# Six pairs instead of four: merged sums on VectorE and a four-slot tile of raw weights in an encoder layer

## The chip, the core and the metric

The kernel runs on one core of a Trainium2 chip. The metric is the device time of one execution in microseconds. TensorE (PE), VectorE (DVE), ScalarE (ACT) and the queue of SyncE (SP), which issues nearly all transfers, work side by side and wait for each other by semaphores. Each takes its own instructions strictly in the order in which the program wrote them.

## What is computed

One encoder layer on x of 256 x 4096. Its two large products are what counts here:

```python
h = layer_norm(x, emb_ln_g, emb_ln_b)
p = h @ w_in                      # 4096 x 13312
y_conv = c_b * centred_short_conv(c_c * c_h, conv_w) * silu(c_z)
y_attn = banded_window_attention(a_q, a_k, a_v, sink) * silu(a_z)
y = concatenate([y_conv, y_attn]) @ w_out     # 4096 x 4096
out = layer_norm(DN_ALPHA * h + y, ln_g, ln_b)
```

All is float32. The attention has 16 query heads in 4 groups and a window of 128 positions to each side.

## The kernel before

**Halves.** A float32 product is made of fast matmuls on rounded numbers. ACT rounds the raw weights `w` to `whi` (`split_hi`, L205), DVE subtracts to get the remainder `wlo` (`split_lo`, L209), and PE sums three products: both halves of x with `whi`, the high half of x with `wlo`. There are three buffers of each half, so PE must have finished a step's matmuls before the halves of the step three later can be made.

**Pieces and pairs.** The weights come in steps. A piece ("s") holds four tiles of 128 rows by 512 columns, 1 MB, and costs PE 48 matmuls of 256 columns (`mm`, L252 for the input, `mm_out`, L926 for the output). A pair ("S") holds two such tiles, 0.5 MB, and uses Strassen's scheme: seven products instead of eight, hence 21 matmuls instead of 24 (`mm_pair`, L277 to L280). For that it needs sums of its weight blocks, which DVE makes (`sums`, L184 to L186: one sum of 512 elements a partition, two of 256), and then halves of seven blocks, 1792 elements, instead of 2048 for a piece. It also needs sums of x or y, made once (`x_sums`, `y_sums`), and the four combined results of a chunk are put together by DVE afterwards (`pair_copy`, `pair_sums`, L682 to L685, then `plus_res`, L934).

**Order of the work.** All engines' orders are written by hand. There is a list of steps, first 26 input chunks, then 9 output chunks (seven of 512 columns, numbered 0 to 6 here, and two of 256, numbers 7 and 8). Input chunks from the fourth on have the pattern `sSShSsSSsSSs` (h is half a piece). Output chunks 0 and 1 have eight pieces, chunks 2 to 6 have `sSsSsSsSss`: six pieces and four pairs. In the round of step j the program writes, in this order: the matmuls of step j, `split_hi` of step j+3, whatever else is due there (the table `later`, filled by `at`), the loads, `sums` of step j+4, and `split_lo` of step j+3.

**Loads.** `loads` gives SP the next weights, at most up to step j+7, if a buffer is free by then: `w0` to `w2`, an extra one in the input part, and idle parts of the result tile `R` in the output part. SP waits for DVE to have split what the buffer held.

**Around an output chunk's start.** When the last matmul of a chunk is done, DVE adds its two results to the residual and takes statistics (`end_out`, L941 and L944). In the first step of the next chunk it multiplies them by the last norm's weight (`end_out2`, L948), which frees the tile `gb`; then SP loads the residual rows of the new chunk (`res_load`, L897 to L901: three rows spread over the partitions into `gb`, two tiles of x into `xc`, 256 KB each). DVE prepares them later in the chunk (`residual`, L907 and L909). In chunk 2, `rows_split` also makes 15 small transfers (L876).

**Attention.** In the input part, PE multiplies the softmax's p, turned and split into halves, with v (`pv`, L621 and L623). DVE makes the low half (`p_lo`, L614).

Of the kernel before, what the change touches and what calls it, by code (L numbers as in the profile page):

```python
# [27 lines left out]
PIECE = HK * P  # L28
# [4 lines left out]
W = 512  # L33
# [7 lines left out]
HW = W // 2  # L41
# [47 lines left out]
def npairs(ci):  # L89
    return PAIRS[ci] if ci < OUT else OUT_ORDERS[ci - OUT].count("S")  # L90

# [3 lines left out]
N_IN = len(IN_STEPS)  # L95
# [6 lines left out]
def encoder_kernel(ctx: ExitStack, tc: tile.TileContext, x, emb_g, emb_b, wi, ws, conv_w, sink, wo, ln_g, ln_b, out):  # L102
    nc = tc.nc
# [20 lines left out]
    raw, wh, wl = {}, {}, {}  # L124
    psc = pw = pc = R = None
    extra = []
    user = {}
    in_R = [(steps.index(("opair", OUT + 4, OP - 1)) + 1, "R0"), (steps.index(("opair", OUT + 4, OP - 1)) + 1, "R1"),
            (steps.index(("opair", OUT + 6, OP - 1)) + 1, "R2")]

    def w_bufs(j):

        bs = [(wpool, f"w{k}") for k in range(N_W)] + (extra if j < N_IN else [])
        if j >= N_IN and R is not None:
            late = j > in_R[0][0]
            bs += [(None, name) for last, name in in_R if j <= last and late == (name == "R2")]
        last_user = lambda b: max(u for c, u in user.items() if c == b or b[1] == "R2" and c[0] is None) if (
            b in user or b[1] == "R2") else -1
        return min((last_user(b), k) for k, b in enumerate(bs)), bs

    def load(j, to=None):
        kind, a, b = steps[j]
        if to is None:
            (_, k), bs = w_bufs(j)
            pool, name = bs[k]
            user[bs[k]] = j
            if pool is None:
                to = raw[j] = {"R0": R[:, 0, D // 2:D], "R1": R[:, 1, D // 2:D], "R2": R[:, :, 3 * D // 4:D]}[name]
            else:
                to = raw[j] = pool.tile([P, PIECE], F32, name=name, bufs=1)  # L150
        src = {"in": (wi, IN_PIECES), "out": (wo, OUT_PIECES)}.get(kind, (ws, ALL_PAIRS))
        src = src[0][src[1].index((a, b))]
        if len(to.shape) == 3:
            if is_pair(j):
                nc.sync.dma_start(out=to[:, 0, :], in_=src)
            else:
                nc.sync.dma_start(out=to, in_=src.rearrange("p (i n) -> p i n", i=2))
        else:
            nc.sync.dma_start(out=to[:, 0:src.shape[1]], in_=src)

    def loads(j):

        nonlocal nxt
        while nxt < len(steps) and nxt <= j + 7:
            (u, _), bs = w_bufs(nxt)
            if u > j + (2 if len(bs) > N_W else 3):
                break
            load(nxt)
            nxt += 1

    def sums(j):
# [12 lines left out]
        nc.vector.tensor_tensor(s01, b22, b12.to_broadcast([P, 2, HW]), op=ALU.add)  # L184
        nc.vector.tensor_tensor(r(6), r(5), r(1), op=ALU.add)  # L185
        nc.vector.tensor_tensor(r(7), r(6), r(3), op=ALU.add)  # L186
# [7 lines left out]
    def half_tile(j, name):  # L194
        if j < len(steps) - 1 and name == "whi":
            return wpool.tile([P, PIECE + GAP], F32R, name=name)[:, OFF:OFF + PIECE]
        if j < len(steps) - 1:
            return wpool.tile([P, PIECE + 2 * OFF], F32R, name=f"{name}{j % 3}", bufs=1)[:, OFF:OFF + PIECE]
        (_, k), bs = w_bufs(j)
        user[bs[k]] = j  # L200
# [29 lines left out]
    for name in ("whi", "w0", "w1", "w2", "wlo0", "m", "nm", "wlo1", "den", "es", "wlo2"):  # L230
        n = {"whi": PIECE + GAP}.get(name, PIECE + 2 * OFF if name[:3] == "wlo" else PIECE if name[0] == "w" else 2)
        wpool.tile([P, n], F32, name=name, bufs={"whi": 3, "m": 4, "nm": 3, "den": 4, "es": 3}.get(name, 1))


    acc = {}
# [58 lines left out]
    with tc.tile_pool(name="pro", bufs=1) as pro:  # L294
# [28 lines left out]
        for j in range(4, 2 + N_W):  # L323
            load(j)

        NQ = KT // 4
# [99 lines left out]
        x_split(3)  # L426
        split(3)
        load(6)
        transp2(4)
        mm(2)  # L430
        turned2(4)
        x_split(4)
        split(4)
        load(7)
        transp2(5)
        mm(3)
        turned2(5)
        x_split(5)
        split(5)
        load(8)  # L440
        transp2(6)
        mm(4)
        turned2(6)
        x_split(6)
        split(6)
        load(9)
        transp2(7)
        mm(5)
        turned2(7)
        x_split(7)  # L450
        split(7)
        load(10)
        mm(6)
        split(8)
        load(11)
        x_split(0)
        split(9)
        load(12)
        x_split(1)
    n_pro = 7  # L460

# [300 lines left out]
    def at(j, fn, *a):  # L762
        later.setdefault(j, []).append((fn, a))
# [33 lines left out]
                at(j + t, f, g, b)  # L797

    c_ch0 = IN_ORDER.index(C_CH)
    nxt = n_pro + 6  # L800
# [61 lines left out]
    first_cols, zt = [], []  # L862

    def rows_load():
        for k, src in enumerate((ln_g, ln_b)):
# [12 lines left out]
    def res_load(n):  # L878
# [5 lines left out]
        if n < ncs - 2:  # L884
            xc = p2.tile([P, 2, W], F32, name="xc")[:, :, 0:w]
        elif n == ncs - 2:
            zt.append(p2.tile([P, 8 * W], F32, name="z", tag="SC"))
            xc = zt[0][:, 6 * W:6 * W + 2 * w].rearrange("p (a b) -> p a b", a=2)
        else:
            z = zt[0]  # L890
            gb = z[:, 0:3 * w].rearrange("p (a b) -> p a b", a=3)
# [246 lines left out]
```

## Time and profile before

| | us |
|---|---|
| median of three runs | 1503.43 (1503.41 to 1503.45) |
| the profiled execution's own time | 1503.42 |
| its span, first to last instruction | 1501.7 |
| PE busy, share of the span | 1488.7 (99%) |
| DVE busy | 1329.3 (89%) |
| ACT busy | 782.0 (52%) |
| granted TensorE clock, mean | 0.999 |

Rows of a timeline read: start in us, duration in us, engine, line, operation, tiles written and read, shape, count, and in brackets the idle time before it and what ended that. Rows of groups give, after the shape and count, the total busy time in us, the mean of one in ns, and the idle time before them with its releasers. "w<-in_ws" is the transfer of a pair's weights, "w<-in_wi" and "w<-in_wo" those of pieces.

### The profile page before, as it was taken

To read this page: it belongs to the slowest core of one execution; us is meant where nothing else is said; L and a number is where in the kernel's file an instruction comes from. 1 tells how busy PE (TensorE), PEld (TensorE's weight loads), DVE (VectorE), ACT (ScalarE), POOL (GpSimd) and SP (SyncE) were. 2 spreads that over 40 slices of the span, in tenths; PEclk is the share of its full clock that TensorE was granted. 3 is DMA by queue.
4 is the path that set the end of the run, shared out by engine and by line. 5 is a ranking of instruction groups with operands and counts; after the bars stand their busy time and mean duration, and the time that the engine had idled before them with its cause. 6 is when DMAs were issued, how large, how long until landed. Compare 5 with 4: busy or idle time off the path is not lost.

```text
span 1501.7 us, 30113 instructions
## 1 busy us (share of the span) xinstructions
PE 1488.7 (99%) x12947; PEld 1473.4 (98%) x12947; DVE 1329.3 (89%) x1555; ACT 782.0 (52%) x669; POOL 1.3 (0%) x7
## 2 busy tenths in 40 slices
PE   7999999999999999999999999999999999999998
PEld 4999999999999999999999999999999999999997
DVE  7768989999899998999899999999999688888876
ACT  5545556657566665544555455555455444444431
POOL 0000000000000000000000000000000000000000
PEclk9999999999999999999999999999999999999999
DMA  7555655656555556657556655656667665666673
GB/s 290 217 182 197 210 197 172 208 185 205 200 184 190 190 185 212 230 188 241 202 191 210 225 201 193 216 185 228 203 211 292 259 204 219 262 218 217 221 260 124
DMA packets 71749, 316.18 MB, mean 211 GB/s; under 512 B 8544, under 2 KB 12608, under 8 KB 50880
## 3 DMA queue, kind: packets, MB, share of 16 engines
q1 hardware_dynamic: 70608, 312.43, 59.5%
q8 instruction: 101, 1.65, 0.4%
q10 hardware_dynamic: 1008, 1.84, 0.3%
q14 instruction: 32, 0.26, 0.1%
HBM read 305.23 MB, written 8.91 MB: 209 GB/s over the span
## 4 chain that ended last, share of the span: by engine, by line
PE 98%; DVE 1%; DMA 0%; ACT 0%; SPq 0%; issue 0%; ACTq 0%
PE acc L252 45%; PE acc L926 20%; PE pacc L278 6%; PE pacc L277 6%; PE pacc L280 6%; PE acc L278 4%; PE acc L277 4%; PE acc L280 4%; PE att L494 1%; DVE st L331 0%; PE att L621 0%; PE att L607 0%; PE acc L381 0%; DMA x<-in_x 0%; PE att L364 0%; DVE x L339 0%
## 5 line engine op out<-in xcount | busy, mean ns | idle before, releaser
L205 ACT ACTIVATE whi<-w 128x2048 fp32r<-128x2048 f32 (+1 forms) x354 | 621.9, 1761 | 590.7 <-DVE w L186 230.4
L209 DVE TENSOR_TENSOR wlo<-w,whi 128x2048 fp32r<-128x2048 f32 (+1 forms) x354 | 736.0, 2083 | 101.0 <-ACT whi L205 84.0
L252 PE MATMUL acc<-whi,xT 128*128 128x256 f32 x3952 | 473.4, 276 | 0.0
L252 PEld LDWEIGHTS acc<-whi,xT 128*128 128x128 f32 x3952 | 459.3, 188 | 0.0
L252 PE MATMUL acc<-wlo,xT 128*128 128x256 f32 x1976 | 245.8, 275 | 0.0
L252 PEld LDWEIGHTS acc<-wlo,xT 128*128 128x128 f32 x1976 | 234.0, 188 | 0.0
L926 PE MATMUL acc<-whi,xT 128*128 128x256 f32 x1696 | 201.8, 275 | 0.0
L926 PEld LDWEIGHTS acc<-whi,xT 128*128 128x128 f32 x1696 | 196.6, 188 | 0.4 <-issue 0.4
L184 DVE TENSOR_TENSOR w<-w 128x512 f32<-128x512 f32 x179 | 122.3, 683 | 7.8 <-DMA w<-in_ws 7.8
L926 PE MATMUL acc<-wlo,xT 128*128 128x256 f32 x848 | 105.3, 275 | 0.0
L277 PE MATMUL acc<-whi,xT 128*128 128x256 f32 x370 | 101.9, 275 | 0.0
L278 PE MATMUL acc<-whi,xT 128*128 128x256 f32 x370 | 101.9, 275 | 0.0
L926 PEld LDWEIGHTS acc<-wlo,xT 128*128 128x128 f32 x848 | 100.4, 188 | 0.0
L277 PE MATMUL pacc<-whi,xT 128*128 128x256 f32 x350 | 97.9, 280 | 0.0
L278 PE MATMUL pacc<-whi,xT 128*128 128x256 f32 x350 | 96.4, 275 | 0.0
L280 PE MATMUL pacc<-wlo,xT 128*128 128x256 f32 x350 | 96.2, 275 | 0.0
L280 PE MATMUL acc<-wlo,xT 128*128 128x256 f32 x370 | 92.8, 275 | 0.0
L277 PE MATMUL pacc<-whi,SC 128*128 128x256 f32 x330 | 90.9, 275 | 0.0
L278 PE MATMUL pacc<-whi,SC 128*128 128x256 f32 x330 | 90.9, 275 | 0.0
L280 PE MATMUL pacc<-wlo,SC 128*128 128x256 f32 x330 | 82.9, 276 | 0.0
L185 DVE TENSOR_TENSOR w<-w 128x256 f32<-128x256 f32 x179 | 76.1, 425 | 6.2
L186 DVE TENSOR_TENSOR w<-w 128x256 f32<-128x256 f32 x179 | 76.1, 425 | 6.2
(218 smaller groups left out, 1673.4 us busy)
## 6 DMA issues: line engine op xcount, KB each, us to landing
w<-in_wi SPq DMA_DIRECT2D x112, 1024.0 KB
w<-in_ws SPq DMA_DIRECT2D x202, 512.0 KB
w<-in_wo SPq DMA_DIRECT2D x41, 1024.0 KB
R<-in_wo SPq DMA_DIRECT2D x13, 1024.0 KB
x<-in_x SPq DMA_DIRECT2D x7, 512.0 KB
yl<-yd SPq DMA_DIRECT2D x7, 512.0 KB
xc<-in_x SPq DMA_DIRECT2D x14, 256.0 KB
R<-in_ws SPq DMA_DIRECT2D x6, 512.0 KB
```

The source lines that it names most:

```text
L184: nc.vector.tensor_tensor(s01, b22, b12.to_broadcast([P, 2, HW]), op=ALU.add)
L185: nc.vector.tensor_tensor(r(6), r(5), r(1), op=ALU.add)
L186: nc.vector.tensor_tensor(r(7), r(6), r(3), op=ALU.add)
L205: nc.scalar.activation(part(j, wh[j]), part(j, raw[j]), AF.Copy)
L209: nc.vector.tensor_tensor(part(j, wl[j]), part(j, raw[j]), part(j, wh[j]).bitcast(F32), op=ALU.subtract)
L252: nc.tensor.matmul(acc[ci, i][:, c:c + HW], x, w[:, k * W + c:k * W + c + HW], start=(first and w is hi and k + off + c == 0), stop=(last ...
L277: nc.tensor.matmul(o, ah, hi[:, w, :], start=(opens and p == 0), stop=False)
L278: nc.tensor.matmul(o, al, hi[:, w, :], start=False, stop=False)
L280: nc.tensor.matmul(o, ah, lo[:, w, :], start=False, stop=(closes and last))
L494: nc.tensor.transpose(ps[:, c, i * P:(i + 1) * P], t[:, i, (2 * b + c) * P:(2 * b + c + 1) * P], ident)
L926: nc.tensor.matmul(acc[ci, i][:, c:c + HW], y, m[:, k * w + c:k * w + c + HW], start=(first and off + c == 0), stop=(last and c + HW == w))
```

## The change

1. Output chunks 2 to 6 have the pattern `sSSsSSsSSss`: five pieces and six pairs (`OP`, `OUT_ORDERS`). The sums of y for six pairs are made in the rounds of steps 6 to 11 of the output part, where those for four were made in steps 9 to 12. Their tile and the tile `z` in the same place grow from 8 to 12 blocks of 512 columns.
2. The three buffers of raw weights become one tile `wall` with four slots. Two pairs that follow each other directly (`couple`) may be loaded into slots only, and their sums are then made together, once, in the round in which those of the first were due: one sum over 2 x 512 elements, two over 2 x 256 (new L192 to L194).
3. A load may go ahead if the step that holds its buffer is at most two steps on, in the prologue three (before, two where there were extra buffers and three elsewhere). In the prologue each load from the seventh on comes one place sooner.
4. The last piece of all is loaded into the tile `z`, and its halves lie in the place of `wall`.
5. The kernel is built with a smaller scratch area for dynamic transfers.

```diff
-OP = 4
-OUT_ORDERS = ["s" * 8] * 2 + ["sSsSsSsSss"] * 5 + ["", ""]
-N_W = 3
+OP = 6
+OUT_ORDERS = ["s" * 8] * 2 + ["sSSsSSsSSss"] * 5 + ["", ""]
+N_W = 4
...
+    def couple(j):
+        return is_pair(j) and j + 1 < len(steps) and is_pair(j + 1) and not (j and couple(j - 1))
+
+    coupled = lambda j: couple(j) or j > 0 and couple(j - 1)
...
-        bs = [(wpool, f"w{k}") for k in range(N_W)] + (extra if j < N_IN else [])
+        bs = [("wall", k) for k in range(N_W)]
+        if coupled(j):
+            return min((user.get(b, -1), k) for k, b in enumerate(bs)), bs
+        bs += extra if j < N_IN else []
...
-            (u, _), bs = w_bufs(nxt)
-            if u > j + (2 if len(bs) > N_W else 3):
+            (u, _), bs = w_bufs(nxt) if nxt < len(steps) - 1 else ((-1, 0), [])
+            if u > j + (2 if j >= n_pro else 3):
                 break
...
     def sums(j):
 
-        if j >= len(steps) or not is_pair(j):
+        if j >= len(steps) or not is_pair(j) or j in summed:
+            return
+        if coupled(j) and j + 1 in in_wall:
+            summed.add(j + 1)
+            a, b = sorted((in_wall[j], in_wall[j + 1]))
+            t = wall[:, a:b + 1:b - a, :].rearrange("p s (b w) -> p s b w", w=HW)
+            nc.vector.tensor_tensor(t[:, :, 4:6, :], t[:, :, 1:3, :], t[:, :, 0:1, :].to_broadcast([P, 2, 2, HW]), op=ALU.add)
+            nc.vector.tensor_tensor(t[:, :, 6, :], t[:, :, 5, :], t[:, :, 1, :], op=ALU.add)
+            nc.vector.tensor_tensor(t[:, :, 7, :], t[:, :, 6, :], t[:, :, 3, :], op=ALU.add)
             return
...
-        return bs[k][0].tile([P, PIECE], F32R, name=bs[k][1], bufs=1)
+        t = wpool.tile([P, 2, 2 * PIECE], F32R, name="wend", tag="wall", bufs=1) if name == "whi" else last_half[0]
+        last_half.append(t)
+        return t[:, int(name == "wlo"), OFF:OFF + PIECE]
...
-        p2.tile([P, 8 * W], F32, name="SC")
+        p2.tile([P, 12 * W], F32, name="SC")
...
     for k in range(OP):
-        at(chunks[1][3] + 1 + k, y_sums, k)
+        at(N_IN + 6 + k, y_sums, k)
...
-    nc = _bacc.Bacc("TRN2", target_bir_lowering=False, num_devices=1)
+    nc = _bacc.Bacc("TRN2", target_bir_lowering=False, num_devices=1, dynamic_dma_scratch_size=1024)
```

**DVE at the start of output chunk 5.** Rows are line, operation, tiles written and read, shape. `wlo` of 1792 are the halves of pairs, of 2048 those of pieces; L948, in the new file L976, is `end_out2`, L944 the end of `end_out`. Before:

```order
L944 BN_STATS s_13769<-R 128x6
L209 TENSOR_TENSOR wlo_15866<-w_15685,whi 128x1792
L948 TENSOR_TENSOR R<-R,gb 128x512 x2
L184 TENSOR_TENSOR w_15801<-w_15801 128x512
L185 TENSOR_TENSOR w_15801<-w_15801 128x256
L186 TENSOR_TENSOR w_15801<-w_15801 128x256
L209 TENSOR_TENSOR wlo_15907<-R,whi 128x2048
L209 TENSOR_TENSOR wlo_15960<-w_15801,whi 128x1792
L184 TENSOR_TENSOR w_15902<-w_15902 128x512
```

After:

```order
L194 TENSOR_TENSOR wall<-wall 128x2x256
L230 TENSOR_TENSOR wlo_15394<-R,whi 128x2048
L976 TENSOR_TENSOR R<-R,gb 128x512 x2
L230 TENSOR_TENSOR wlo_15430<-wall,whi 128x1792
L230 TENSOR_TENSOR wlo_15457<-wall,whi 128x1792
L192 TENSOR_TENSOR wall<-wall 128x2x512
L193 TENSOR_TENSOR wall<-wall 128x2x256
L194 TENSOR_TENSOR wall<-wall 128x2x256
L230 TENSOR_TENSOR wlo_15513<-wall,whi 128x2048
```

Two halves of pairs now follow `end_out2` directly, and then the merged sums of the third couple (steps 7 and 8 of the chunk).

**SP at the same place.** `in_ws` are a pair's weights, `in_wo` a piece's; `gb` and `xc` are the residual loads. Before:

```order
L159 DMA w_15864<-in_wo 128x2048
L897 DMA gb<-in_emb_g_row 128x512
L898 DMA gb<-in_emb_b_row 128x512
L899 DMA gb<-in_ln_g 128x512
L901 DMA xc<-in_x 128x512 x2
L159 DMA w_15902<-in_ws 128x1024
L157 DMA R<-in_wo 128x2x1024
```

After:

```order
L172 DMA wall<-in_ws 128x1024
L925 DMA gb<-in_emb_g_row 128x512
L926 DMA gb<-in_emb_b_row 128x512
L927 DMA gb<-in_ln_g 128x512
L929 DMA xc<-in_x 128x512 x2
L172 DMA wall<-in_ws 128x1024
L170 DMA R<-in_wo 128x2x1024
```

The load in front of the residual loads is now the first pair of the third couple (step 7), the one behind them its second (step 8); before, the load behind them was the pair of step 7, the last of the four.

**DVE in the attention part**, around the later of two low halves of p near the end of a group of heads (`kp<-att,kp`, L614, in the new file L638). Before:

```order
L627 TENSOR_TENSOR zT<-att,zT 128x256
L184 TENSOR_TENSOR w_3445<-w_3445 128x512
L185 TENSOR_TENSOR w_3445<-w_3445 128x256
L186 TENSOR_TENSOR w_3445<-w_3445 128x256
L209 TENSOR_TENSOR wlo_3549<-w_3409,whi 128x2048
L614 TENSOR_TENSOR kp<-att,kp 128x512
L184 TENSOR_TENSOR w_3488<-w_3488 128x512
```

After:

```order
L651 TENSOR_TENSOR zT<-att,zT 128x256
L192 TENSOR_TENSOR wall<-wall 128x2x512
L193 TENSOR_TENSOR wall<-wall 128x2x256
L194 TENSOR_TENSOR wall<-wall 128x2x256
L230 TENSOR_TENSOR wlo_3451<-wall,whi 128x2048
L638 TENSOR_TENSOR kp<-att,kp 128x512
L230 TENSOR_TENSOR wlo_3485<-wall,whi 128x1792
```

The sums of the later pair, which stood behind the low half, are now made together with those of the earlier one in front of it.

More of the change, by code (lines that the diff above doesn't have):

```diff
@@ L142, in load @@
         kind, a, b = steps[j]
-        if to is None:
+        if to is None and j == len(steps) - 1:
+            to = raw[j] = z_tile()[:, 8 * W:12 * W]
+        elif to is None:
             (_, k), bs = w_bufs(j)
@@ L146, in load @@
             user[bs[k]] = j
-            if pool is None:
+            if pool == "wall":
+                to = raw[j] = wall[:, name, :]
+                in_wall[j] = name
+            elif pool is None:
                 to = raw[j] = {"R0": R[:, 0, D // 2:D], "R1": R[:, 1, D // 2:D], "R2": R[:, :, 3 * D // 4:D]}[name]
@@ L229, in encoder_kernel @@
     const.tile([P, 8], F32, name="gap")
-    for name in ("whi", "w0", "w1", "w2", "wlo0", "m", "nm", "wlo1", "den", "es", "wlo2"):
-        n = {"whi": PIECE + GAP}.get(name, PIECE + 2 * OFF if name[:3] == "wlo" else PIECE if name[0] == "w" else 2)
-        wpool.tile([P, n], F32, name=name, bufs={"whi": 3, "m": 4, "nm": 3, "den": 4, "es": 3}.get(name, 1))
+    for name in ("whi", "wall", "wlo0", "m", "nm", "wlo1", "den", "es", "wlo2"):
+        n = {"whi": PIECE + GAP}.get(name, PIECE + 2 * OFF if name[:3] == "wlo" else N_W * PIECE if name == "wall" else 2)
+        t = wpool.tile([P, n], F32, name=name, bufs={"whi": 3, "m": 4, "nm": 3, "den": 4, "es": 3}.get(name, 1))
+        if name == "wall":
+            wall = t.rearrange("p (s n) -> p s n", s=N_W)
     acc = {}
@@ L322, in encoder_kernel @@
         nc.sync.dma_start(out=sk, in_=bass.AP(tensor=sink.tensor, offset=sink.offset, ap=[[0, P], [1, HEADS]]))
-        for j in range(4, 2 + N_W):
+        for j in range(4, 5):
             load(j)
@@ L428, in encoder_kernel @@
         load(6)
+        load(7)
         transp2(4)
@@ L433, in encoder_kernel @@
         split(4)
-        load(7)
+        load(8)
         transp2(5)
@@ L439, in encoder_kernel @@
         split(5)
-        load(8)
+        load(9)
         transp2(6)
@@ L445, in encoder_kernel @@
         split(6)
-        load(9)
+        load(10)
         transp2(7)
@@ L451, in encoder_kernel @@
         split(7)
-        load(10)
+        load(11)
         mm(6)
         split(8)
-        load(11)
+        load(12)
         x_split(0)
         split(9)
-        load(12)
+        load(13)
         x_split(1)
@@ L862, in encoder_kernel, with z_tile @@
     first_cols, zt = [], []
+    def z_tile():
+        if not zt:
+            zt.append(p2.tile([P, 12 * W], F32, name="z", tag="SC"))
+        return zt[0]
     def rows_load():
@@ L886, in res_load @@
         elif n == ncs - 2:
-            zt.append(p2.tile([P, 8 * W], F32, name="z", tag="SC"))
-            xc = zt[0][:, 6 * W:6 * W + 2 * w].rearrange("p (a b) -> p a b", a=2)
+            xc = z_tile()[:, 6 * W:6 * W + 2 * w].rearrange("p (a b) -> p a b", a=2)
         else:
```

9 lines of the change are left out of this document (4 added, 5 removed).

## The prediction

> **What bounds the kernel now.** I read the page's busy line first, then the waits of PE, the chain of work, and the windows of one output chunk.
>
> ```profile
> span 1501.7 us, 30113 instructions
> PE 1488.7 (99%) x12947; PEld 1473.4 (98%) x12947; DVE 1329.3 (89%) x1555; ACT 782.0 (52%) x669; POOL 1.3 (0%) x7
> ```
> ```profile
> PE att L394 <- DMA x<-in_x: 8.4, 1, 8.4
> PE att L986 <- ACT lhs L968: 0.4, 1, 0.4
> ```
> ```profile
> 1305.96 16.32 PE acc L926 x144
> 1348.12 16.32 PE acc L926 x144
> ```
> PE waits twice, at the start and at the end, and in between issues one matmul every 16.32 us / 144 = 113.3 ns. The two rows of the chain lie one output chunk apart: 42.16 us, which is 372 matmuls at that rate (six pieces of 48, four pairs of 21). So every matmul taken away is worth its full 113.3 ns, as long as the other engines keep up. DVE is the one to look at. The rows are stretches, with the busy time of PE, PEld, DVE and ACT:
>
> ```profile
> core 0: us, PE busy (x) PEld busy (x) DVE busy (x) ACT busy (x) POOL busy (x), PEclk, DMA share, GB/s
> 1150.00:1200.00 50.00, 50.00 (x443) 50.00 (x443) 35.32 (x31) 22.25 (x16) 0.00 (x0) 1.00 0.75 281
> 1322.28:1364.44 42.16, 42.16 (x374) 42.16 (x374) 36.70 (x38) 18.66 (x11) 0.00 (x0) 1.00 0.62 207
> ```
> In one output chunk with pairs (second row) DVE is busy for 36.70 of 42.16 us and has 5.46 us free. That is the reserve which this change draws on.
>
> **The change part by part.** *Matmuls.* In each of five chunks two pairs (2 x 21) take the place of one piece (48): 5 x 6 = 30 matmuls fewer, 30 x 113.3 ns = **-3.40 us**. PE then needs 366 x 113.3 ns = 41.48 us a chunk.
>
> *DVE's work in such a chunk.* Durations by shape:
>
> ```profile
> L209 DVE TENSOR_TENSOR wlo<-w,whi 128x1792 fp32r<-128x1792 f32 x179 | 361.1, 2020 | 49.0 <-ACT whi L205 39.1 <-PE acc L926 9.1 <-PE att L568 0.7
> L209 DVE TENSOR_TENSOR wlo<-w,whi 128x2048 fp32r<-128x2048 f32 x152 | 347.4, 2287 | 45.3 <-ACT whi L205 44.9
> L697 DVE TENSOR_TENSOR ug<-ug,tm 128x1024 f32<-128x1024 f32 x7 | 8.5, 1219 | 0.0
> L948 DVE TENSOR_TENSOR R<-R,gb 128x512 f32<-128x512 f32 x14 | 9.0, 684 | 0.0
> ```
> and a stretch of its timeline at the start of the next chunk:
>
> ```profile
> 1366.49 1.29 DVE L948 TENSOR_TENSOR R<-R,gb 128x512 f32<-128x512 f32 x2
> 1367.69 0.68 DVE L184 TENSOR_TENSOR w<-w 128x512 f32<-128x512 f32 x1
> 1368.41 0.42 DVE L185 TENSOR_TENSOR w<-w 128x256 f32<-128x256 f32 x1
> 1368.87 0.42 DVE L186 TENSOR_TENSOR w<-w 128x256 f32<-128x256 f32 x1
> 1369.21 2.28 DVE L209 TENSOR_TENSOR wlo<-R,whi 128x2048 fp32r<-128x2048 f32 x1
> 1372.36 2.03 DVE L209 TENSOR_TENSOR wlo<-w,whi 128x1792 fp32r<-128x1792 f32 x1 [0.87 <-PE acc L926]
> 1377.33 0.69 DVE L184 TENSOR_TENSOR w<-w 128x512 f32<-128x512 f32 x1 [2.94 <-DMA w<-in_ws]
> ```
> Three sums of one pair take 1369.21 - 1367.69 = 1.52 us, and an operation that doesn't depend on the one in front starts 0.08 us before that ends (L209 at 1369.21, L186 to 1369.29). Two pairs merged are one sum of 1024 elements and two of 512; by the rows of these sizes 1.22 + 0.68 + 0.68 = 2.58 us, 0.46 us less than 2 x 1.52. Per chunk: three merged sums for four single ones, 7.74 - 6.08 = +1.66; two more halves of 1792, 2 x 1.94 = +3.88; one half of 2048 less, -2.21. Together +3.33, so 40.03 us of DVE work where PE needs 41.48. The reserve is down to 1.45 us.
>
> *The new wait.* At the first step of a chunk DVE finishes L948, and SP, which waited for that, issues the five residual loads of 256 KB and only then the next weights:
>
> ```profile
> 1367.80 0.33 SPq L897 DMA_DIRECT2D gb<-in_emb_g_row  x1
> 1369.12 0.91 SPq L901 DMA_DIRECT2D xc<-in_x  x2
> 1370.13 0.45 SPq L159 DMA_DIRECT2D w<-in_ws  x1
> ```
> ```profile
> 1370.00:1372.00 2.00, 2.00 (x20) 2.00 (x20) 1.50 (x1) 1.47 (x1) 0.00 (x0) 1.00 0.73 124
> 1376.00:1377.30 1.30, 1.30 (x13) 1.30 (x13) 0.00 (x0) 0.00 (x0) 0.00 (x0) 1.00 1.04 429
> ```
> The pair of weights behind them was used at 1377.33, the moment it landed: 9.55 us after L948 ended (1367.78). DVE stood 2.94 us for it, unseen by PE, because it had 5.46 us to give. After the change the load in that place is the second half of the third couple (the loop of loads reaches seven steps ahead, so at the chunk's first step it stops one short of it), and the merged sums need it. The order shows what DVE has between L948 and these sums: two halves of 1792, 3.88 us. So it stands 9.55 - 3.88 = 5.67 us, with the next halves queued behind the waiting sums, and PE and ACT wait for those. It is a loop, since the loads start when DVE ends L948: one round costs DVE 40.03 + 5.67 = 45.70 us against PE's 41.48, so a chunk takes **4.22 us longer** than its matmuls; five such chunks +21.1. Between 0 (the wait fits into the 1.45) and 28 us (all of 5.67 lost each time) I take what the sum gives. The Trainium skill's page "DMA: Bandwidth & Descriptors" (Anatomy of one DMA) fits a DMA as 2.0 us plus its bytes at 436 GB/s: 1.84 MB would land after 6.2 us, an estimate by that page of the skill, and the five chunks would lose some 4 us. The rows show 124 GB/s in the second stretch after the issue and 429 only later; I go by them.
>
> DVE enters the first of these chunks ahead of PE; this lead is between 0 and the 5.46 us for which it waits in a chunk, I take 2: -2.0.
>
> *The fifteen small row loads.* They are issued late in chunk 2, and the next couple's second half, then the residual loads, stand behind them.
>
> ```profile
> 1272.60 11.60 SPq L876 DMA_DIRECT2D rows<-R  x15
> ```
> ```profile
> 1310.27 0.42 DVE L683 TENSOR_TENSOR R<-pacc,R 128x256 f32<-128x256 f32 x1
> 1311.53 1.28 DVE L934 SCALAR_TENSOR_TENSOR R<-xc,R 128x512 f32<-128x512 f32 x2
> 1361.43 0.68 DVE L941 TENSOR_TENSOR R<-acc,R 128x512 f32<-128x512 f32 x1
> 1362.15 0.69 DVE L944 BATCH_NORM_STATS2 s<-R 128x6 f32<-128x512 f32 x1
> ```
> Until the sums that need it DVE has four sums of products (4 x 0.45), L934 twice (1.28), two halves (3.88) and L941/L944 twice (2.7): 9.7 us. The load is issued 11.6 us after the first of the rows and takes between 0.52 MB / 429 GB/s = 1.2 us and the 7.2 us of the load above that stood behind five others; alone it should be nearer the lower end, I take 3. DVE stands for 11.6 + 3 - 9.7 = 5 us, once: **+5.0** (0 to 5).
>
> *The attention part.* PE needs p's low half (L614) soon after it is made:
>
> ```profile
> 311.08 0.68 DVE L614 TENSOR_TENSOR kp<-att,kp 128x512 fp32r<-128x512 f32 x1
> 574.29 0.68 DVE L614 TENSOR_TENSOR kp<-att,kp 128x512 fp32r<-128x512 f32 x1
> 312.81 0.61 PE L621 MATMUL att<-kp,v 128*128 128x256 f32 x4
> 575.41 0.39 PE L623 MATMUL att<-kp,v 128*128 128x256 f32 x2
> 307.36 0.68 DVE L184 TENSOR_TENSOR w<-w 128x512 f32<-128x512 f32 x1
> 305.13 0.33 SPq L159 DMA_DIRECT2D w<-in_ws  x1
> ```
> The leads are 312.81 - 311.76 = 1.05 and 575.41 - 574.97 = 0.44 us. At the second place a merged sum of 2.58 stands in front of L614 where one of 1.52 stood: 1.06 more, 0.6 beyond the lead. At the first, the merged sums have come forward to 307.36 - 1.52 = 305.84 in DVE's time, and their second load, now issued at 305.13, is not there before 306.4 by the 1.2 us above. A wait of 1.6 us takes 0.6 beyond the lead. Five such places in the four groups of heads: **+3.0** (0 to 5).
>
> *At nothing:* two more sums of y (about 2.3 us each) and one step sooner fall into chunks 0 and 1, where DVE has 14.7 of 50 us free (first window row); without that cover they would cost 4.6. ACT has half its time free. The fourth slot lets the fifth piece's load start without waiting for a split, and PE's start hangs on x alone. The last piece's halves go into the slots' tile and must wait for the split before it, which DVE makes three pieces of 5.44 us ahead of PE; at worst 2.3. The smaller scratch only makes room.
>
> **How the numbers follow.** The profiled execution took 1503.42 us, 1.7 more than its span, the median is 1503.43. 1503.42 - 3.40 + 21.1 - 2.0 + 5.0 + 3.0 = **1527.1 us**, slower by 1.6%. About 0.2% (3.0 us) is what a measurement of this kernel can tell from no change. Chance 0.75.
>
> **The rivals.** *DVE keeps up* (the other side). The halves are made three steps ahead of PE, and the wait of 2.94 us above was swallowed before. If the couples' waits are swallowed as well, 1500.0 us remains, or 1503.0 with the attention part's 3.0. It turns at 1.45 us of wait a chunk. Against it: 5.67 is four times that, and comes back in every chunk, where a lead can be spent only once. Chance 0.07 (faster 0.05, same 0.02).
>
> *The wait stays as it was,* 2.94 us, because weights come sooner with four slots. A round is then 42.97 us, five chunks lose 7.4: 1503.42 - 3.40 + 7.4 - 2.0 + 5.0 + 3.0 = 1513.4. Against it: slots don't move the load ahead of the residual loads in SP's order. The fit of the Trainium skill's page above speaks for it. Chance 0.11.
>
> *The clock falls in the stalls.* PE would stand for 3 to 5 us at a time inside a chunk. After PE thinned out at the end of the program the granted clock fell:
>
> ```profile
> 14.00:20.00 6.00, 6.00 (x21) 1.00 1.04 419
> 1495.00:1501.70 6.70, 2.65 (x7) 0.79 0.74 277
> ```
> (PE's busy time, granted clock, DMA share, GB/s.) If it halves after each of six stalls for about 3.4 us, 1.7 us are lost each, 10 in all: 1537. Against it: with DVE setting the pace PE has 4.2 us a chunk to make that good. The Trainium skill's page "TensorE: Matmul & The Clock Gate" (Part 1) says that a window of about 3.4 us without work halves the clock, which these stalls would only just reach. Chance 0.07.
>
> The change does what it says: the order shows 85 merged sums and 30 matmuls fewer. The likeliest case alone runs from 1515.6 (attention and rows 0, lead 5.5) to 1531 (both 5, lead 0); the clock's case goes on to 1537. Range 1514 to 1537, which leaves out the first rival and half of the second. Slower 0.93, same 0.02, faster 0.05.
>
> **What would show it.** Right: PE waits that are new, at L954 and L303 (the low halves' matmuls in the new file) for DVE's half, 4 to 5 us in each of chunks 2 to 6; DVE waiting at L192 for a DMA of weights, 5 to 6 us five times, over 30 us in all; five residual loads ahead of that load on SP; chunks of 45 to 46 us; short PE waits at the two pv lines for L638. Wrong: chunks of 41.5 us, or DVE's waits at L192 as long as forecast and PE without a gap; then the lead is larger than I think. Waits of PE for ACT, or a granted clock under 1.00 inside the output part, would mean another cause.

## The result and the profile after

| | us |
|---|---|
| before, median of four runs | 1503.44 (1503.41 to 1503.49) |
| changed, median of four runs | 1531.16 (1529.93 to 1534.86) |
| ratio | 1.0188, 95% interval 1.0176 to 1.0200 |
| changed, the profiled execution: own time, span | 1531.03, 1529.0 |

The forecast was 1527.1 us in a range of 1514 to 1537. The change makes the kernel 1.9% slower. The busy line and then the waits of PE and of DVE in the changed kernel:

```profile
PE 1497.7 (98%) x12917; PEld 1479.3 (97%) x12917; DVE 1321.4 (86%) x1347; ACT 785.5 (51%) x676; POOL 1.3 (0%) x7
```
```profile
PE acc L954 <- DVE wlo L230: 14.9, 6, 3.4
...
PE pacc L303 <- DVE wlo L230: 1.4, 2, 0.7
PE att L645 <- DVE kp L638: 1.1, 3, 0.4
PE att L647 <- DVE kp L638: 0.9, 2, 0.5
```
```profile
DVE wall L192 <- DMA wall<-in_ws: 30.8, 10, 7.4
...
DVE wall L192 <- issue: 11.2, 3, 5.9
```
PE has 30 matmuls fewer and is nevertheless busy for 9.0 us longer (1497.7 against 1488.7): with 3.4 us of work gone, 12.4 us went into slower matmuls. Its new waits sum to 18.3 us, all for DVE. 18.3 + 12.4 - 3.4 = 27.3 us is the whole growth of the span. DVE in its turn waits at the first of the merged sums, L192, for weights.

The stretch of DVE's timeline from chunk 2's start shows where (start, duration, and in brackets the idle time before and what ended it):

```profile
1245.93 1.29 DVE L976 TENSOR_TENSOR R<-R,gb 128x512 f32<-128x512 f32 x2
...
1258.52 1.22 DVE L192 TENSOR_TENSOR wall<-wall 128x1024 f32<-128x1024 f32 x1 [7.43 <-DMA wall<-in_ws]
...
1294.65 1.22 DVE L192 TENSOR_TENSOR wall<-wall 128x1024 f32<-128x1024 f32 x1 [4.97 <-DMA wall<-in_ws]
...
1299.44 1.29 DVE L976 TENSOR_TENSOR R<-R,gb 128x512 f32<-128x512 f32 x2
...
1310.14 1.23 DVE L192 TENSOR_TENSOR wall<-wall 128x1024 f32<-128x1024 f32 x1 [5.54 <-DMA wall<-in_ws]
...
1345.09 1.28 DVE L976 TENSOR_TENSOR R<-R,gb 128x512 f32<-128x512 f32 x2
...
1356.10 1.23 DVE L192 TENSOR_TENSOR wall<-wall 128x1024 f32<-128x1024 f32 x1 [5.85 <-DMA wall<-in_ws]
...
1391.06 1.28 DVE L976 TENSOR_TENSOR R<-R,gb 128x512 f32<-128x512 f32 x2
...
1402.07 1.23 DVE L192 TENSOR_TENSOR wall<-wall 128x1024 f32<-128x1024 f32 x1 [5.85 <-issue]
...
1437.11 1.29 DVE L976 TENSOR_TENSOR R<-R,gb 128x512 f32<-128x512 f32 x2
...
1447.36 1.23 DVE L192 TENSOR_TENSOR wall<-wall 128x1024 f32<-128x1024 f32 x1 [5.09 <-issue]
```
From L976 to L976 the chunks take 53.51, 45.65, 45.97 and 46.05 us where PE's matmuls need 41.48. Each has one wait of 5 to 7 us two halves after L976, and chunk 2 a second one at its end. ("issue" as releaser means that the profile shows nothing; it is the same place in the same order.) SP in chunk 3 shows what the late load stands behind:

```profile
1300.76 0.33 SPq L925 DMA_DIRECT2D gb<-in_emb_g_row  x1
...
1303.09 0.36 SPq L172 DMA_DIRECT2D wall<-in_ws  x1
```
L925 is issued when L976 is done (1300.73), the five residual loads follow, and the couple's second half is issued at 1303.09 and used at 1310.14, 9.4 us after L976.

### The profile page after: what moved, and what is told of

The parts are those of the page before. It is cut to its first block, busy times and chain, and to the rows that moved or that the text cites. A ratio compares the mean times of both kernels' runs of the same rounds, so it can differ in the third digit from the quotient of the medians.

```text
span 1529.0 us, 29832 instructions
## 1 busy us (share of the span) xinstructions
PE 1497.7 (98%) x12917; PEld 1479.3 (97%) x12917; DVE 1321.4 (86%) x1347; ACT 785.5 (51%) x676; POOL 1.3 (0%) x7
## 4 chain that ended last, share of the span: by engine, by line
PE 86%; DVE 8%; issue 2%; DMA 2%; SPq 1%; ACT 0%; DVEq 0%; ACTq 0%
PE acc L275 44%; PE acc L954 12%; PE pacc L300 5%; PE pacc L301 5%; PE pacc L303 5%; DVE wlo L230 4%; PE acc L301 4%; PE acc L300 4%; PE acc L303 4%; DMA wall<-in_ws 2%; DVE wall L192 1%; PE att L518 1%; DVE wall L193 1%; DVE st L354 0%; PE att L631 0%
## 5 line engine op out<-in xcount | busy, mean ns | idle before, releaser
L226 ACT ACTIVATE whi<-wall 128x1792 fp32r<-128x1792 f32 (+1 forms) x289 | 503.8, 1756 | 475.7 <-DVE wall L194 202.8
L230 DVE TENSOR_TENSOR wlo<-wall,whi 128x1792 fp32r<-128x1792 f32 (+1 forms) x289 | 596.2, 2077 | 57.9 <-ACT whi L226 54.7
L275 PEld LDWEIGHTS acc<-whi,xT 128*128 128x128 f32 x3952 | 459.3, 188 | 0.0
L275 PEld LDWEIGHTS acc<-wlo,xT 128*128 128x128 f32 x1976 | 234.0, 188 | 0.0
L226 ACT ACTIVATE whi<-w 128x2048 fp32r<-128x2048 f32 (+1 forms) x74 | 129.2, 1746 | 146.6 <-PE acc L275 107.8
L230 DVE TENSOR_TENSOR wlo<-w,whi 128x2048 fp32r<-128x2048 f32 (+1 forms) x74 | 152.8, 2065 | 49.1 <-ACT whi L226 37.4
L954 PEld LDWEIGHTS acc<-whi,xT 128*128 128x128 f32 x1536 | 178.0, 188 | 0.4 <-issue 0.4
L192 DVE TENSOR_TENSOR wall<-wall 128x1024 f32<-128x1024 f32 x85 | 103.5, 1218 | 42.1 <-DMA wall<-in_ws 30.8
L954 PEld LDWEIGHTS acc<-wlo,xT 128*128 128x128 f32 x768 | 96.4, 198 | 16.0 <-DVE wlo L230 16.0
L300 PE MATMUL pacc<-whi,xT 128*128 128x256 f32 x360 | 101.1, 281 | 0.0
L301 PE MATMUL pacc<-whi,xT 128*128 128x256 f32 x360 | 99.6, 277 | 0.0
```

The costliest lines, as they stand in the source:

```text
L192: nc.vector.tensor_tensor(t[:, :, 4:6, :], t[:, :, 1:3, :], t[:, :, 0:1, :].to_broadcast([P, 2, 2, HW]), op=ALU.add)
L226: nc.scalar.activation(part(j, wh[j]), part(j, raw[j]), AF.Copy)
L230: nc.vector.tensor_tensor(part(j, wl[j]), part(j, raw[j]), part(j, wh[j]).bitcast(F32), op=ALU.subtract)
L275: nc.tensor.matmul(acc[ci, i][:, c:c + HW], x, w[:, k * W + c:k * W + c + HW], start=(first and w is hi and k + off + c == 0), stop=(last ...
L300: nc.tensor.matmul(o, ah, hi[:, w, :], start=(opens and p == 0), stop=False)
L301: nc.tensor.matmul(o, al, hi[:, w, :], start=False, stop=False)
```

## The experiments

All edits are to the changed kernel. "Before" beside an experiment is the kernel before on the same chip, 1503.45 to 1503.55 us.

### Residual loads one step later

```diff
-                if n < ncs - 1:
-                    res_load(n)
+            if t == 1 and n and n < ncs - 1:
+                res_load(n)
```

> The changed kernel (1531.2 us) with one thing moved: the five residual loads are issued one step later, so on SP they stand behind the second half of the third couple. Theory (DVE waits for that half because it stands behind the residual loads): the wait of 5 to 7 us at L192 in each of chunks 2 to 6 goes; a chunk is then bound by PE's 41.48 us, as DVE's work is 40.03. What stays is the wait of about 5 us behind the fifteen row loads and the attention part's 4 us: 1503.4 - 3.4 + 4 + 2 to 5 = 1506 to 1509 us. First rival (DVE simply has too much to do with six pairs): chunks stay at 45 to 46 us, 1529 to 1532. Second rival (the granted clock, 0.993 in the changed kernel, is lost for a reason of its own): some 10 us of loss remain, 1515 to 1520.

1514.38 us (ratio 1.0073, 1.0058 to 1.0088), 16.8 us less than the changed kernel, but not down to 1509. DVE's timeline from chunk 3 on:

```profile
1293.52 1.28 DVE L976 TENSOR_TENSOR R<-R,gb 128x512 f32<-128x512 f32 x2
...
1333.56 1.28 DVE L976 TENSOR_TENSOR R<-R,gb 128x512 f32<-128x512 f32 x2
...
1374.23 1.28 DVE L976 TENSOR_TENSOR R<-R,gb 128x512 f32<-128x512 f32 x2
...
1385.26 1.23 DVE L192 TENSOR_TENSOR wall<-wall 128x1024 f32<-128x1024 f32 x1 [5.87 <-issue]
...
1420.22 1.29 DVE L976 TENSOR_TENSOR R<-R,gb 128x512 f32<-128x512 f32 x2
```
Chunk 3 takes 40.04 us without a wait, which is DVE's bare work; chunk 4 takes 40.67, with 0.45 us of small waits for ACT and PE and none at L192; chunk 5 has the wait of 5.87 and takes 45.99. What differs is the order on SP. In chunk 3 the half is issued ahead of the first residual load (L925 at 1294.84), in chunk 5 behind it (L925 at 1375.55):

```profile
1377.87 0.43 SPq L172 DMA_DIRECT2D wall<-in_ws  x1
```
In chunks 5 and 6 the half may be loaded only when the round of the chunk's third step comes, since no slot is free before that, so that it still stood behind the moved loads there. I had overlooked this; the expectation took all five chunks as mended. So this one kernel holds the effect with and without its cause.

### Residual loads and residual two steps later

```diff
-                if n < ncs - 1:
-                    res_load(n)
-            if t == (0 if n == ncs - 1 else 2 if n == ncs - 2 else 4 if n else 7):
+            if n and n < ncs - 1 and t == (2 if npairs(OUT + n) else 0):
+                res_load(n)
+            if t == (0 if n == ncs - 1 else 2 if n == ncs - 2 else 6 if npairs(OUT + n) else 4 if n else 7):
```

> The changed kernel with the residual loads two steps later and their preparation on DVE two steps later: in all of chunks 2 to 6 the third couple's second half now stands ahead of them on SP; moved by one step only, that was so in chunks 2, 3 and 4 alone, because in 5 and 6 the half could not be loaded before a slot came free a step later. Theory: in 2 to 4 no wait; in 5 and 6 the half waits for its slot (about 2 us after the residual step) and lands some 3 us later, a wait of 1 to 1.5 us, which fits into DVE's reserve of 1.45: another 8 us less than 1514.4, so 1505.5 to 1508.5 us, what stays being the input part's 4 us and the rows. Rival (in 5 and 6 the slot, not the order on SP, makes the half late): 1511 to 1515.

1509.43 us (ratio 1.0041, 1.0028 to 1.0055), just above the expected span. What is left at L192 in chunk 2 and in chunk 5:

```profile
1289.60 1.23 DVE L192 TENSOR_TENSOR wall<-wall 128x1024 f32<-128x1024 f32 x1 [4.77 <-DMA wall<-in_ws]
...
1384.32 1.23 DVE L192 TENSOR_TENSOR wall<-wall 128x1024 f32<-128x1024 f32 x1 [1.53 <-DMA wall<-in_ws]
```
The wait behind the row loads is untouched; in chunks 5 and 6 the slot holds the half back for 1.5 and 1.6 us, which costs PE nothing. PE waits once in the output part, 2.9 us. So the order on SP is worth 21.7 us.

### The same order, but loads that need not wait for DVE

```diff
-            gb = p2.tile([P, 3, w], F32, name="gb")
+            gb = p2.tile([P, 2, w], F32, name="gb")
+            lg = p2.tile([P, w], F32, name=f"lg{n % 2}")
...
-        nc.sync.dma_start(out=gb[:, 2, :], in_=bcast(ln_g, c0, w))
+        nc.sync.dma_start(out=lg, in_=bcast(ln_g, c0, w))
...
-        nc.vector.tensor_tensor(r, r, res[n][0][:, 2, :], op=ALU.mult)
+        nc.vector.tensor_tensor(r, r, res[n][2], op=ALU.mult)
```

> The changed kernel in which the spread row of the last norm's weight, the one that the residual step on DVE (end_out2) reads, has two tiles of its own; the rest of gb is as before. All five residual loads keep their bytes and their place on SP, ahead of the late half, but they need not wait for end_out2 any more and start some 9 us sooner. Theory (the loop matters: DVE's step starts the loads, and DVE then waits for what stands behind them): no wait in chunks 2 to 4 and 1 to 1.5 us in chunks 5 and 6, where the half's slot comes free only after that step; as in the kernel with the loads moved behind the couple, 1506 to 1510 us. Rival (the bytes ahead of the half count, wherever they start, and the run with three loads was fast because it moved less): waits of 2.5 to 5 us in each chunk, 1515 to 1528 us.

1507.21 us (ratio 1.0024, 1.0015 to 1.0034). SP and DVE at the start of chunk 3:

```profile
1286.46 0.43 SPq L927 DMA_DIRECT2D gb<-in_emb_g_row  x1
```
```profile
1293.08 1.29 DVE L978 TENSOR_TENSOR R<-R,lg 128x512 f32<-128x512 f32 x2
...
1299.33 1.23 DVE L192 TENSOR_TENSOR wall<-wall 128x1024 f32<-128x1024 f32 x1 [1.09 <-DMA wall<-in_ws]
```
All five loads still stand ahead of the half, with all their bytes, but they start 6.6 us before DVE's step and not 1.3 us behind its start. The wait shrinks to 1.09 us in chunk 3, where none was expected; there is none in chunks 2 and 4, and 1.44 us in 5 and 6. So the order alone does no harm: it is the loop, in which DVE's step releases the loads and DVE then waits for what is behind them.

### Sums of each pair alone

```diff
-        if coupled(j) and j + 1 in in_wall:
+        if False and coupled(j) and j + 1 in in_wall:
```

> The changed kernel with the merging switched off: six pairs, four slots, the same loads, but the sums of each pair are made alone, those of a couple's second pair one round later. DVE has 3 x 0.46 = 1.4 us more to do in each chunk (41.4 against PE's 41.5 us). Theory: the sums that need the load behind the residual loads now have two sums of one pair (3.0), two halves of pairs (3.9) and one of a piece (2.2) in front of them, 9.1 us after the residual step for a load that lands after some 9.5 us, so the wait falls from 5.7 to about 0.5 us, and the wait behind the row loads goes as well: 1500 to 1504 us, below the kernel before or beside it. Rival (DVE's amount of work decides): slower than the changed kernel by 5 x 1.4 = 7 us, 1538.

1502.37 us (ratio 0.9993, 0.9984 to 1.0003): the same as before, and 29 us faster than with merged sums (some 4 of them in the input part, see below), though DVE has more work. The sums that need the late half, in chunk 4:

```profile
1326.73 1.29 DVE L976 TENSOR_TENSOR R<-R,gb 128x512 f32<-128x512 f32 x2
...
1337.64 0.69 DVE L205 TENSOR_TENSOR wall<-wall 128x512 f32<-128x512 f32 x1 [0.43 <-DMA wall<-in_ws]
```
The half comes as late as ever (9.6 us after L976), but the sums that need it stand one round later, so the wait is 0.43 us (0.30 to 1.10 in the other chunks that have one). The amount of DVE's work falls as an explanation; what counts is when the order asks for the second half. The merging itself brings the harm, by asking for both halves at the earlier of two times.

### Fewer matmuls in three chunks

```diff
             for k in range(k0, k1 or pk):
                 s = q * pk + k
+                if m is lo and 3 <= n <= 5 and k != pk - 1:
+                    continue
```

> The changed kernel with 60 matmuls (6.8 us) left out in each of output chunks 3, 4 and 5: of the products with the low half of a piece's weights three tiles in four are skipped, so the output is less exact; DVE's and SP's orders are untouched. Theory (DVE's round of work and wait, 45.7 us, sets the pace there, and the time that PE loses to a lower clock only fills its gaps): PE waits about 20 us more, and the time stays within 3 us of the changed kernel's, 1528 to 1532. Rival (the 10 us that PE loses to the clock lie on the path, PE sets the pace between the gaps): 10 to 20 us less, 1511 to 1521.

1533.98 us (ratio 1.0206, 1.0191 to 1.0221): no gain from 180 matmuls (20.4 us) less, rather 2.8 us more, and 2 us above the expected span. PE's waits in the pieces, and DVE from chunk 3 on:

```profile
PE acc L956 <- DVE wlo L230: 31.8, 8, 6.0
...
PE pacc L303 <- DVE wlo L230: 2.5, 4, 0.8
```
```profile
1299.08 1.28 DVE L978 TENSOR_TENSOR R<-R,gb 128x512 f32<-128x512 f32 x2
...
1345.20 1.29 DVE L978 TENSOR_TENSOR R<-R,gb 128x512 f32<-128x512 f32 x2
```
PE's waits for low halves grow from 16.3 to 34.3 us, nearly what was taken away, and the chunk takes 46.12 us. PE doesn't set the pace there, and so time that it loses to a lower clock isn't on the path either.

### Row transfers spread out

The list `row_dmas` takes what `rows_split` issued, three are issued in each of steps 2 to 6 of chunk 3. The inserted lines also pull a small ACT operation that followed `rows_split` (0.20 us, on 128 x 1) into the same five steps, where it runs five times; ACT is busy for about half of the time.

```diff
-                    nc.sync.dma_start(out=rows[b + r:b + r + 1, 0:n * P].bitcast(F32), in_=hl[a0:a0 + n, h, :].bitcast(F32))
+                    row_dmas.append((rows[b + r:b + r + 1, 0:n * P].bitcast(F32), hl[a0:a0 + n, h, :].bitcast(F32)))
...
+            if n == 3 and t in (2, 3, 4, 5, 6):
+                for _ in range(3):
+                    o, i_ = row_dmas.pop(0)
+                    nc.sync.dma_start(out=o, in_=i_)
```

> The changed kernel with the fifteen row transfers taken out of chunk 2 and issued three at a time in five steps of chunk 3 (the split of the rows stays in chunk 2). Theory: DVE's wait of 4.97 us at L192 at the end of chunk 2 goes, as the couple's second half no longer stands behind 11.6 us of issues, and three rows at a time (2.3 us) fall where SP has nothing urgent: the waits behind the residual loads stay at 5 to 7 us. 1531.2 - 5 = 1525 to 1528 us. Rival (a couple's load is late there for want of a slot, not for the rows): 1530 to 1532.

1526.93 us (ratio 1.0157, 1.0141 to 1.0172), 4.2 us less, and the wait at the end of chunk 2 is gone:

```profile
1257.34 1.23 DVE L192 TENSOR_TENSOR wall<-wall 128x1024 f32<-128x1024 f32 x1 [6.26 <-DMA wall<-in_ws]
...
1293.20 1.29 DVE L978 TENSOR_TENSOR R<-R,gb 128x512 f32<-128x512 f32 x2
```

### No merging in the input part

```diff
-        if coupled(j) and j + 1 in in_wall:
+        if j >= N_IN and coupled(j) and j + 1 in in_wall:
```

> The changed kernel with merging switched off in the input part only. Theory: the input part loses nothing any more (the first matmul of the output part at 1144.5 to 1145 us instead of 1148.5, no waits at the two pv lines), the output part is as it was: 1531.2 - 4 = 1526.5 to 1528 us. Rival (the lead that DVE and the loads bring into the output part is what the input part's delay gave it, so that the output part then loses more): 1529 to 1531.

1529.12 us (1527.77 to 1530.80; ratio 1.0171, 1.0157 to 1.0185): the median lies just inside the rival's range (from 1529), the four runs on both sides of its edge. The first weight load of the output part, in the kernel before, in the changed one and here (the first of the two starts in each row):

```profile
L926 PEld LDWEIGHTS acc<-whi,xT x1696: 187/188/192, 1144.3 to 1484.3; 128*128 128x128 f32 x189
```
```profile
L954 PEld LDWEIGHTS acc<-whi,xT x1536: 186/188/192, 1148.2 to 1511.8; 128*128 128x128 f32 x192
```
```profile
L954 PEld LDWEIGHTS acc<-whi,xT x1536: 187/188/192, 1144.5 to 1508.3; 128*128 128x128 f32 x192
```
The input part lost 3.9 us by the merging and has 3.7 of them back; the last weight load also comes 3.5 us sooner, so that in this execution the output part does not lose more, as the rival would have it. The execution (1527.92 us) is one of the two faster ones, though. In the medians only 2.0 us are seen, with ranges that overlap; the rest I can't place, and the rival is not excluded.

### Why the half lands so late

Three runs take away part of what could slow its landing. The first takes the spread rows from 128 different rows of x:

```diff
-        nc.sync.dma_start(out=gb[:, 0, :], in_=bcast(emb_gr, c0, w))
-        nc.sync.dma_start(out=gb[:, 1, :], in_=bcast(emb_br, c0, w))
-        nc.sync.dma_start(out=gb[:, 2, :], in_=bcast(ln_g, c0, w))
+        for k in range(3):
+            nc.sync.dma_start(out=gb[:, k, :], in_=x[(k % 2) * P:(k % 2 + 1) * P, c0:c0 + w])
```

> The changed kernel with the three loads of rows spread over all partitions (gb, 256 KB each) taken from 128 different rows of x instead of one row each: same count, size, place and tile, other data, so the output is not the layer's. If only the order and the size of what stands ahead matter, the couple's second half still lands 9 to 10 us after the residual step, DVE waits 5 to 6 us and the time stays at 1529 to 1532. If reading one row 128 times is what makes these loads slow (124 GB/s after their issue in the kernel before, 429 for other transfers), that half lands after 6 to 7 us, the wait falls to 2 to 3 us, each round to 42.5 to 43 us, and the time to 1513 to 1518.

1527.34 us (ratio 1.0161, 1.0144 to 1.0178), 1.7 us below the first expectation and far from the second. In chunk 3 the half lands 8.8 us after the residual step (L975 ends at 1298.50) and the wait is

```profile
1307.31 1.23 DVE L192 TENSOR_TENSOR wall<-wall 128x1024 f32<-128x1024 f32 x1 [4.94 <-DMA wall<-in_ws]
```
Two of the microseconds in which those loads move, in the changed kernel and then here (the last three columns are the granted clock, the share of the transfer engines and GB/s):

```profile
1303.00:1304.00 1.00, 0.58 0.62 141
1304.00:1305.00 1.00, 1.00 0.68 117
```
```profile
1300.00:1301.00 1.00, 0.59 0.90 281
1301.00:1302.00 1.00, 1.00 0.97 352
```
Reading one row 128 times is slower, less than half the rate in these windows, but that is worth only 0.6 us of the landing. The second run empties the loads behind the half (n is the output chunk, t the step in it):

```diff
-        if len(to.shape) == 3:
...
+        if kind == "out" and 2 <= n <= 7 and (t in (9, 10) and n < 7 or t == 0 and n > 2):
+            if len(to.shape) == 3:
+                nc.sync.dma_start(out=to[:, :, 0:32], in_=src.rearrange("p (i n) -> p i n", i=2)[:, :, 0:32])
+            else:
+                nc.sync.dma_start(out=to[:, 0:64], in_=src[:, 0:64])
+        elif len(to.shape) == 3:
```

> The changed kernel, in which the piece loads that SP issues right behind the late half of the third couple (two of the chunk's pieces and the next chunk's first, 1 MB each) move only one part in 32 of their bytes, so that the pieces are computed from stale weights and the output is not the layer's; what stands ahead of the late half is untouched. In the changed kernel that half lands 9 to 12 us after the residual step. If it is late because the loads behind it take a share of the transfer engines, it now lands after about 6.2 to 7 us, DVE waits 2 to 3 us, rounds of 42.5 to 43 us, 1513 to 1518 us. If the loads ahead of it alone make it late, it lands after 9 to 9.7 us as before, DVE waits 5 to 6 us, and the time stays at 1528 to 1532.

1530.99 us (ratio 1.0186, 1.0171 to 1.0202), and in chunk 3

```profile
1308.94 1.23 DVE L198 TENSOR_TENSOR wall<-wall 128x1024 f32<-128x1024 f32 x1 [5.69 <-DMA wall<-in_ws]
```
The half lands 9.6 us after the residual step, so here what is issued behind it doesn't delay it. The windows of this run show the course: 115 to 174 GB/s from 1300 to 1304, 299 to 420 from 1304 to 1307, then 215 and 51 until the half is used at 1308.94. The slow start is what the first run took away, but there the loads behind were full. The two edits were not run together, so each may hide a part of what the other would give. The third run leaves two of the five loads out:

```diff
-            gb = p2.tile([P, 3, w], F32, name="gb")
+            gb = res[1][0] if 2 <= n <= 6 else p2.tile([P, 3, w], F32, name="gb")
...
-        nc.sync.dma_start(out=gb[:, 1, :], in_=bcast(emb_br, c0, w))
-        nc.sync.dma_start(out=gb[:, 2, :], in_=bcast(ln_g, c0, w))
+        if not 2 <= n <= 6:
+            nc.sync.dma_start(out=gb[:, 1, :], in_=bcast(emb_br, c0, w))
+            nc.sync.dma_start(out=gb[:, 2, :], in_=bcast(ln_g, c0, w))
```

> The changed kernel with three residual loads instead of five in chunks 2 to 6 (two of the three spread rows are left as they were, so the output is not the layer's): 0.79 MB instead of 1.31 stand ahead of the late half, and two issues of 0.47 us less. If what stands ahead sets its landing, at the rate of the changed kernel (1.31 + 0.52 MB in 9.5 us, 0.19 MB a us), it lands 2.7 us sooner, DVE waits 2.5 to 3.5 us, rounds of 42.5 to 43.5 us, 1515 to 1520 us. If the half's own transfer with what is issued behind it sets it, only the issues count: 0.9 us sooner, waits of 4.5 to 5, 1525 to 1528 us.

1506.14 us (ratio 1.0018, 1.0009 to 1.0027), far below both expectations, and not for the reason given there:

```profile
1286.58 0.43 SPq L925 DMA_DIRECT2D gb<-in_emb_g_row  x1
```
```profile
1293.21 1.28 DVE L977 TENSOR_TENSOR R<-R,gb 128x512 f32<-128x512 f32 x2
```
With the last norm's row left in place, nothing is loaded any more into what DVE's step reads, and the loads start 6.6 us ahead of it. The run says nothing on sizes; it broke the loop. The run with the tile of its own, above, was made to check this with all bytes in place, and it agrees within 1.1 us.

### All three places mended

The edits of the two-step, the row and the input experiment together.

> The changed kernel with all three places mended: residual loads and their preparation two steps later, row transfers three at a time in chunk 3, no merging in the input part; six pairs and merged sums in the output part stay. If the three terms are all there is, the 30 matmuls saved are what remains: 1500 to 1501.5 us, faster than the kernel before (1503.5) by 0.15 to 0.25%. If DVE's load of 40.0 out of 41.5 us leaves too little slack for the rest, 1502 to 1506.

1500.13 us (1499.76 to 1500.97) beside 1503.55: ratio 0.9978, 0.9969 to 0.9986. PE waits for nothing but the start's x and the end:

```profile
PE att L417 <- DMA x<-in_x: 8.5, 1, 8.5
PE att L1016 <- ACT lhs L998: 0.4, 1, 0.4
```
This version beats both kernels, by what the 30 matmuls are worth. The other parts of the change (the rule for loading ahead, the place of the last piece, the scratch area) are still in it, so they cost nothing that shows. The same with no merged sums anywhere:

> All three places mended as in the kernel that reached 1500.1 us, but without merged sums anywhere: DVE has 41.4 us of work in a chunk instead of 40.0, PE 41.5. If the merged sums are not needed for the six pairs, 1499.5 to 1500.8 us, the same. If DVE needs their 1.4 us of slack a chunk to ride out small delays, PE waits some 0.2 to 0.5 us a chunk: 1501 to 1503 us.

1500.85 us (1500.05 to 1502.04; ratio 0.9983, 0.9974 to 0.9992). PE waits once for DVE in the output part, 0.7 us. The two can't be told apart: six pairs need the loads in time, not the merging.

## Why the prediction was right

**Matmuls, -3.4 us.** Right: with all waits gone the mended kernel is 3.4 us below the kernel before.

**DVE's work and the wait, the main term.** Right in mechanism and place. DVE's chunks are its work plus its wait: 45.97 - 5.85 = 40.12 us of work for a forecast of 40.03. The waits were 7.43, 5.54, 5.85, 5.85 and 5.09, 29.8 us together for 5 x 5.67 = 28.4. Only the first is well off, and in other runs that same place shows 6.26 (above). The wait of 2.94 us (the second rival) didn't come. Of the 9.4 us until the half lands, 0.6 are the spread rows and nothing is what is queued behind, each taken away alone; what makes up the rest stays open. The estimate by the Trainium skill's page "DMA: Bandwidth & Descriptors" (Anatomy of one DMA) was 6.2 us; the trace doesn't agree, and it decides. That section of the Trainium skill gives the fit for one transfer on GpSimd's path; here six went out in a row on SP's queue, so the estimate stretched it.

**The lead, -2.0, and the rows, +5.0.** The rows' wait was 4.97, and spreading them out gave 4.2. No run isolates the lead. Not counted were DVE's four small operations in `rows_split` (L901 and L902, 1.0 us together), which lie on the path once DVE sets the pace.

**The attention part, +3.0.** Measured 3.9 at the first weight load of the output part, the mechanism as forecast: PE waits at the two pv lines for L638, 2.0 us. Of the other 1.9 us, 1.7 show as busy time of the same 9877 matmuls (1137.5 us against 1135.8 before) at a granted clock of 1.00; why they take longer is open.

**The terms at nothing.** PE has no wait between the output part's start and chunk 2, so the sums of y cost nothing there, and the mended kernel leaves no room for the others.

**The sum.** 4.1 us were missing to 1531.16: 0.9 from the input part, 1.4 from the waits, 1.0 from the rows' operations, and 0.4 if DVE's work is 0.09 us above the forecast in each of the five chunks make 3.7; 0.4 remain unplaced.

**Where a statement failed.** PE was to wait 4 to 5 us in each of chunks 2 to 6, and a granted clock under 1.00 inside the output part was to mean another cause. Neither holds. The windows by chunk (PE's busy time, granted clock, DMA share, GB/s) and PE's waits in chunks 3, 4 and 5:

```profile
1300.00:1345.00 45.00, 41.63 (x329) 0.89 0.59 217
1345.00:1391.00 46.00, 43.83 (x384) 1.00 0.57 212
1391.00:1437.00 46.00, 42.80 (x352) 0.93 0.59 212
```
```profile
1315.07 3.78 PE L954 MATMUL acc<-wlo,xT 128*128 128x256 f32 x16 [3.37 <-DVE wlo L230]
...
1361.04 2.12 PE L954 MATMUL acc<-wlo,xT 128*128 128x256 f32 x16 [1.48 <-DVE wlo L230]
...
1407.00 3.79 PE L954 MATMUL acc<-wlo,xT 128*128 128x256 f32 x16 [3.20 <-DVE wlo L230]
```
After each of the four longest stalls (2.96 and 3.22 us behind DVE's two waits of chunk 2, and the 3.37 and 3.20 above) the clock is halved for a while, PE falls further behind, and at the next chunk it has less to wait: 3.37, 1.48, 3.20. The chunks take 45.65, 45.97 and 46.05 us whatever the clock was (0.89, 1.00, 0.93). So the third rival's mechanism was there, and PE's matmuls in the output part did take 10.7 us longer (the rival's sum had 10), but its price was nil, as the run with fewer matmuls shows: DVE sets the pace, and a slower PE only fills its gaps. As a sign of another cause the clock was a bad choice; it is a consequence.

**The first rival,** that DVE keeps up, is what happens when the half comes in time: its 1500.0 us is the mended kernel's 1500.1.

## What to carry to other kernels

When an operation is merged with a later one, it is due at the earlier time and ready at the later one; look up what the later input stands behind on its queue before counting what the merging saves. An engine with a few per cent of slack swallows a wait for a load only if the load's start doesn't hang on that same engine: where it does, the wait returns in every round, and starting the load ahead of the engine's step (another tile, another place in the order) was worth more here than making the loads faster. And when one engine waits for another, look whose round equals work plus wait, here DVE's, before charging the slower clock of the one that waits.

## What the runs showed of the hardware

The granted clock reacts to single stalls. Around PE's wait of 3.37 us in the changed kernel:

```profile
1312.00:1314.00 2.00, 0.00 (x0) 1.00 0.98 414
1314.00:1316.00 2.00, 0.93 (x4) 0.52 0.90 373
```
In windows of half a microsecond the clock falls 2.4 us into this stall and stays at 0.50 for about 6.8 us. After the stalls of 2.96, 3.22 and 3.20 us it is at 0.50 for about 3.4, 3.4 and 6.8 us; after the wait of 1.48 us and shorter ones it stays at 1.00. The Trainium skill's page "TensorE: Matmul & The Clock Gate" (Part 1) names an idle window of about 3.4 us for the halving and as long a busy one for the return; the halvings here lasted once or twice that length, but stalls a little shorter than it were enough.

Loads that read one row 128 times moved 117 and 141 GB/s where loads of the same size from 128 rows moved 281 and 352, each in the first microseconds behind their issue (the windows above).
